# Triangular solve in a DeltaNet block: substitution on 16x16 blocks, joined by matrix products

## The chip, the cores and the metric

The kernel runs on one NeuronCore of a Trainium2 chip. The metric is the device time of one launch in microseconds (us); lower is better. The engines are TensorE (PE in the profile, with PEld for its weight loads), VectorE (DVE), ScalarE (ACT), GpSimd (POOL) and SyncE (SP), which issues most of the DMAs. Each engine works through its own instructions in a fixed order and waits on semaphores for the others.

## What is computed

The reference is one layer of a hybrid block: a gated DeltaNet branch and a Fourier branch over 256 tokens (with 256 context tokens before them), a merge, and a mixture of 32 experts. The change concerns one step of the DeltaNet branch. For every chunk of 64 tokens, every one of 8 heads and both directions, a unit lower triangular 64x64 matrix is solved:

```python
lower = jnp.where(strict, bc[..., :, None] * kk * decay, 0.0)
rhs = jnp.concatenate([bc[..., None] * vc, (bc * jnp.exp(gc))[..., None] * kc], axis=-1)
sol = lax.linalg.triangular_solve(jnp.eye(CHUNK) + lower, rhs, left_side=True, lower=True, unit_diagonal=True)
```

With 8 chunks, 8 heads and 2 directions that is 128 matrices. The kernel forms their inverses (transposed, the tiles `ub`) once, and the scan over the chunks then multiplies by them.

## The kernel before

The program goes through these stages: modulation and norm of the inputs (to about 60 us); the projections of the K heads, with their products and decays, which give the strictly triangular matrices in two pages `ah[0]` and `ah[1]`, one for each direction (to about 118 us); the projections of the eight V heads, beside which the triangular matrices are inverted; the four Q heads; the scan over 4 + 4 chunks, with the remaining projections (z, Fourier, gates) as fill between its steps; the merge; the router; and from about 470 us the experts, whose weights (3 x 32 matrices of 4 MB) stream in over the SP queue.

One V head (lines 557 to 571) takes one pass over four engines: ACT rounds the raw weights to `hi` (L156), POOL subtracts for `lo` (L157), PE makes 48 products into a bank `ps_pj` (L164 to L166; the pool has two such banks), ACT starts the convolution (L388), DVE adds its ten other taps (L391, called a tap below), ACT applies SiLU (L405), PE transposes in four pieces (L569), ACT copies them out (L571). A Q head does the same with 24 products and eight taps, and no transposes.

The inversion stands after the V heads in the code, and the scheduler that lays down the program mixes it into them. A 64x64 matrix is cut into four 32x32 blocks. L647 brings the two diagonal blocks of every matrix to one page `xc`, L649 transposes it in 32x32 blocks into `xt`, so that each of the 128 partitions holds two of the 32x32 triangles along its free dimension. The substitution (L651 to L657) then inverts them all at once in 31 steps; step s has two DVE instructions, each on two blocks of 31-s rows by s+1 columns:

```python
V.tensor_tensor(out=pv, in0=tt[:, :, s, 0:s + 1]..., in1=xt[:, :, s, s + 1:32]..., op=ALU.mult)   # L654
V.tensor_tensor(out=tv, in0=tv, in1=pv, op=ALU.subtract)                                         # L657
```

Four transposes (L672, L674) bring the inverses and their transposes back to `uc` (the page `xt`) and `tb` (the page `xc`). ACT spreads the diagonal blocks into `ub` (L678, eight copies). The off-diagonal 32x32 block is the product of three: for each half of the matrices (s = 0, 1), 64 small products of 32x32 (L688) go to a bank `ps_sc` (four such banks, shared with the transposes of the V heads), ACT copies with a minus sign to `yt` (L689), 64 more products (L696) follow, and DVE adds the result to `ub` (L699, twice). The products of the scan's first step (L745) read `ub`. A set below means 64 such small products.

What sets the order: each engine's order is fixed when the program is built. The program's scheduler chose it; buffers (two `ps_pj`, four `ps_sc`, three `a`) and data set when each instruction may start.

Of the kernel before, what the change touches and what calls it, by code (L numbers as in the profile page):

```python
# [14 lines left out]
AF = mybir.ActivationFunctionType  # L15
ALU = mybir.AluOpType
# [29 lines left out]
_o = 0  # L46
for _n, _w in (("ident", 128), ("before", 128), ("ones", 1), ("iota", 64), ("pid", 1),
               ("mle", 128), ("mge", 128), ("mgt", 128), ("mlt", 128), ("par0", 1), ("par1", 1), ("cgt", 64), ("clt", 64), ("ceq", 64),
               ("cle", 64), ("cge", 64), ("ev", 1), ("od", 1), ("sel", 32), ("cc", 128), ("sc", 128), ("cl", 1024)):
    _C[_n] = (_o, _w)  # L50
    _o += _w
NCST = _o
# [3 lines left out]
def _constants():  # L56
    a = np.zeros((128, NCST), np.float32)

    def put(n, v):
        o, w = _C[n]  # L60
        a[:, o:o + w] = v
# [17 lines left out]
    put("cge", tl >= j)  # L79
    put("ev", (t // 32) % 2 == 0)  # L80
    put("od", (t // 32) % 2 == 1)
    put("sel", (t % 32) == np.arange(32)[None, :])
    put("before", t < i)
    put("ones", 1.0)
# [13 lines left out]
def hybrid_block(es: ExitStack, tc: tile.TileContext, cst, x, c, ctx, c_ctx, w_mod, b_mod, norm1_g, norm2_g, w_in,  # L98
# [17 lines left out]
    def P(tag):  # L116
        return ps.tile([128, 512], F32, name="ps_" + tag, tag=tag, bufs=_nb[tag])
# [10 lines left out]
    def page(name, dtype=F32, tag="pg"):  # L128
        return pg.tile([128, 2048], dtype, name=name, tag=tag, bufs=NPG if tag == "pg" else 2)
# [306 lines left out]
    tt = page("tt").rearrange("p (d i c) -> p d i c", d=2, i=32)  # L436
    G.memset(tt.rearrange("p d i c -> p (d i c)"), 0.0)
    G.memset(tt.rearrange("p d i c -> p d (i c)")[:, :, 0:1024:33], 1.0)
# [201 lines left out]


    xc = page("xc").rearrange("p (d m j) -> p d m j", d=2, j=32)
    xt = page("xt").rearrange("p (d j i) -> p d j i", d=2, j=32)
    prod = page("prod")
    for d in range(2):
# [3 lines left out]
        V.transpose(xt[:, d].rearrange("p j i -> p (j i)") if d == 0 else xt[:, d].rearrange("p i j -> p j i"),  # L649
                    xc[:, d].rearrange("p m j -> p j m"))  # L650
    for s in range(31):  # L651
        n = 31 - s
        pv = prod[:, 0:2 * n * (s + 1)].rearrange("p (d i c) -> p d i c", d=2, i=n)
        V.tensor_tensor(out=pv, in0=tt[:, :, s, 0:s + 1].rearrange("p d (o c) -> p d o c", o=1).broadcast_to([128, 2, n, s + 1]),  # L654
                        in1=xt[:, :, s, s + 1:32].rearrange("p d (i o) -> p d i o", o=1).broadcast_to([128, 2, n, s + 1]), op=ALU.mult)
        tv = tt[:, :, s + 1:32, 0:s + 1]
        V.tensor_tensor(out=tv, in0=tv, in1=pv, op=ALU.subtract)  # L657

    take(fz, NZ)
# [4 lines left out]
    zT = page("zT", F32R).rearrange("p (q g t) -> p q g t", q=2, g=4)  # L664


    tb, yt = xc, prod[:, 0:1024].rearrange("p (m n) -> p m n", n=32)
    uc = xt.rearrange("p d j i -> p d (j i)").rearrange("p d (m i) -> p d m i", i=32)
    ub = [page("ub0").rearrange("p (d m n) -> p d m n", d=2, n=64), page("ub1").rearrange("p (d m n) -> p d m n", d=2, n=64)]
    vv = [(tt[:, d].rearrange("p i c -> p (i c)"), tt[:, d].rearrange("p i c -> p c i")) for d in range(2)]  # L670
    for d in range(2):
        V.transpose(uc[:, d].rearrange("p m i -> p i m"), vv[d][d])  # L672
    for d in range(2):
        V.transpose(tb[:, d].rearrange("p m c -> p c m"), vv[d][1 - d])  # L674
    for s in range(2):
        for d in range(2):
            for b in range(2):
                A.activation(ub[s][:, d, :, 32 * b:32 * b + 32], uc[:, d, 16 * s:16 * s + 16, :], AF.Copy, scale=par32[b])  # L678
    for s in range(2):
        p = P("sc")  # L680
        pv = p.rearrange("p (m n) -> p m n", n=32)
        for ml in range(16):
            m = 16 * s + ml
            for d in range(2):
                for hh in range(2):
                    k0 = 64 * hh + 32 * (1 - d)
                    o0 = 64 * hh + 32 * d
                    mm(pv[o0:o0 + 32, ml, :], ah[d][k0:k0 + 32, m, 32 * d:32 * d + 32], uc[k0:k0 + 32, d, m, :], start=True, stop=True)  # L688
        A.activation(yt[:, 16 * s:16 * s + 16, :], pv, AF.Copy, scale=-1.0)  # L689
        p = P("sc")  # L690
        pv = p.rearrange("p (m n) -> p m n", n=32)
        for ml in range(16):
            m = 16 * s + ml
            for q in range(4):
                r = slice(32 * q, 32 * q + 32)
                mm(pv[r, ml, :], tb[r, q % 2, m, :], yt[r, m, :], start=True, stop=True)  # L696
# [548 lines left out]
```

## Time and profile before

| | us |
|---|---|
| median of three runs | 1448.76 (1446.08 to 1449.28) |
| the profiled execution, its own time | 1448.83 |
| its span in the trace | 1446.9 |
| DVE busy over the span | 510.8 (35%) |
| PE busy over the span | 1303.9 (90%) |
| the 62 instructions of the substitution, L654 and L657, DVE busy | 48.7 |
| first product of the scan (L745) starts at | 224.7 |
| DMA moves 418 GB/s in the stretch | 470 to 1420 |

The profile says for each engine when it was busy, and for each wait what released it. A share over the whole span says little here, since the stages have different limits: the engine that sets the pace has to be read stage by stage.

### The profile page before, as it was taken

How to read it: one execution, taken by the hardware profiler on the slowest of the kernel's cores; microseconds unless marked ns; L12 is line 12 of the kernel's file. 1: busy time of each engine (PE TensorE's matmuls, PEld its weight loads, DVE VectorE, ACT ScalarE, POOL GpSimd, SP SyncE). 2: the span in 40 equal slices, each digit the busy share in tenths (PEclk: the TensorE clock that was granted, in tenths of full speed). 3: DMA queues.
4: the chain of work that ended last, by engine and by line, in shares of the span. 5: the costliest groups of instructions: out<-in, count | busy, mean ns of one | idle time of the engine just before them, and what ended most of it. 6: DMA issues, size and time to landing. Idle time of an engine off the chain costs nothing. (4 is left out here: it accounts for less than half of the span.)

```text
span 1446.9 us, 18887 instructions
## 1 busy us (share of the span) xinstructions
PE 1303.9 (90%) x7761; PEld 664.9 (46%) x7761; DVE 510.8 (35%) x965; ACT 243.7 (17%) x434; POOL 276.6 (19%) x256
## 2 busy tenths in 40 slices
PE   4997859899779889999999999999999999999996
PEld 2667858578569634333333333233333333333331
DVE  3579994655348411225112111211121112111213
ACT  3443333233224200000000000000000000000001
POOL 2434336544233130000100000001000000010000
PEclk9998979999879899999999999999999999999999
DMA  9962222124336999999999999999999999999994
GB/s 323 377 249 74 73 60 75 45 78 112 88 131 223 397 406 418 420 398 419 420 421 421 421 421 421 422 420 421 421 421 421 421 421 421 422 420 421 420 422 201
DMA packets 121159, 469.74 MB, mean 325 GB/s; under 512 B 10302, under 2 KB 63782, under 8 KB 69872
## 3 DMA queue, kind: packets, MB, share of 16 engines
q1 hardware_dynamic: 119696, 466.44, 81.0%
q10 hardware_dynamic: 1088, 1.89, 0.4%
q8 instruction: 62, 1.02, 0.3%
q0 software_dynamic: 288, 0.19, 0.2%
q14 instruction: 25, 0.20, 0.0%
HBM read 467.44 MB, written 1.05 MB: 324 GB/s over the span
## 5 line engine op out<-in xcount | busy, mean ns | idle before, releaser
L1111 PE MATMUL ps_gu<-we,xg 128*64 128x512 f32 x2048 | 469.6, 598 | 0.0
L1111 PEld LDWEIGHTS ps_gu<-we,xg 128*64 128x64 f32 x2048 | 141.2, 137 | 293.4 <-issue 280.2
L1134 PE MATMUL ps_dn<-we,aT 128*64 128x512 f32 x1024 | 237.3, 600 | 0.7 <-SPq L1146 0.4
L1100 POOL CAST rowsel<-pick 128x128 fp32r<-128x128 f32 x32 | 9.7, 304 | 684.5 <-PE ps_gu L1112 684.5
L157 POOL TENSOR_TENSOR lo<-raw,hi 128x1024 fp32r<-128x1024 f32 x44 | 106.3, 2418 | 157.6 <-ACT hi L156 123.2
L1143 DVE TENSOR_TENSOR x_pg<-x_pg,ps_st 128x512 f32<-128x512 f32 x128 | 82.6, 685 | 125.7 <-PE ps_st L1141 125.7
L1134 PEld LDWEIGHTS ps_dn<-we,aT 128*64 128x64 f32 x1024 | 66.9, 136 | 120.5 <-issue 113.7
L1117 ACT ACTIVATE sg<-gt 128x512 f32<-128x512 f32 x32 | 20.1, 629 | 448.1 <-DVE gt L1115 423.6
L1119 DVE TENSOR_SCALAR up<-ps_gu 128x512 f32<-128x512 f32 x32 | 22.1, 691 | 196.0 <-PE ps_gu L1112 189.2
L1137 DVE TENSOR_TENSOR ys<-ps_dn,g2r 128x512 f32<-128x512 f32 x32 | 22.1, 692 | 195.9 <-PE ps_dn L1134 195.9
L1141 PE MATMUL ps_st<-ys,wT 64*128 64x512 f32 x256 | 77.3, 641 | 12.8 <-DVE ys L1137 12.0
L156 ACT CAST hi<-raw 128x1024 fp32r<-128x1024 f32 x64 | 66.9, 1047 | 124.5 <-PE ps_pf L165 38.1
L164 PE MATMUL ps_pj<-u,hi 128*128 128x256 f32 x224 | 68.8, 310 | 18.1 <-DVE a L391 18.1
L1126 ACT COPY aT<-ps_tp 128x512 f32<-128x512 f32 x32 | 18.8, 586 | 322.0 <-PE ps_tp L1124 322.0
L1083 PEld LDWEIGHTS ps_tp<-oh,h 128*128 128x128 f32 x512 | 64.6, 201 | 14.1 <-issue 13.3
L391 DVE SCALAR_TENSOR_TENSOR a<-ps_pj,cvw,a 128x189 f32<-128x189 f32 (+3 forms) x152 | 63.8, 432 | 18.0 <-ACT a L388 16.3
L1083 PE MATMUL ps_tp<-oh,h 128*128 128x128 f32 x512 | 68.9, 290 | 1.1 <-DVE oh L1070 1.1
L1115 DVE TENSOR_SCALAR gt<-ps_gu 128x512 f32<-128x512 f32 x32 | 22.2, 692 | 133.2 <-issue 95.4
L165 PE MATMUL ps_pj<-u,hi 128*128 128x256 f32 x224 | 68.8, 308 | 0.0
L166 PE MATMUL ps_pj<-u,lo 128*128 128x256 f32 x224 | 67.2, 301 | 0.0
L1121 POOL TENSOR_TENSOR up<-up,sg 128x512 f32<-128x512 f32 x32 | 40.4, 1263 | 96.1 <-DVE up L1120 96.1
L164 PEld LDWEIGHTS ps_pj<-u,hi 128*128 128x128 f32 x224 | 46.0, 207 | 25.6 <-issue 23.8
(352 smaller groups left out, 1663.7 us busy)
## 6 DMA issues: line engine op xcount, KB each, us to landing
we<-in_w_gate_dram SPq DMA_DIRECT2D x128, 1024.0 KB, 18.4
we<-in_w_up_dram SPq DMA_DIRECT2D x128, 1024.0 KB, 17.8
we<-in_w_down_dram SPq DMA_DIRECT2D x128, 1024.0 KB, 18.9
raw<-in_w_in_dram SPq DMA_DIRECT2D x44, 512.0 KB, 4.0
wmb<-in_w_mod_dram SPq DMA_DIRECT2D x16, 1024.0 KB, 12.8
wm<-in_w_mod_dram SPq DMA_DIRECT2D x16, 512.0 KB, 8.1
raw<-in_w_gdn_out_dram SPq DMA_DIRECT2D x8, 512.0 KB, 4.1
raw<-in_w_merge_out_dram SPq DMA_DIRECT2D x8, 512.0 KB, 3.5
```

The lines of the kernel that those rows point to most:

```text
L156: A.copy(hi, r)
L157: eng.tensor_tensor(out=lo, in0=r, in1=hi.bitcast(F32), op=ALU.subtract)
L164: mm(out_, sh_, mh_, start=start and i == 0, stop=False)
L165: mm(out_, sh_, ml_, start=False, stop=False)
L166: mm(out_, sl_, mh_, start=False, stop=stop and i == n - 1)
L391: V.scalar_tensor_tensor(out=ov, in0=iv, scalar=wap, in1=ov, op0=ALU.mult, op1=ALU.add)
L1083: mm(p[:, kl * n:(kl + 1) * n], h2[:, t, rows2(k)], oh[:, n * t:n * t + n], start=(t == 0), stop=(t == 1))
L1111: mm(p[64 * g:64 * g + 64, :], xg[:, k, :], w[:, 512 * g:512 * g + 512], start=(k == 0), stop=False)
L1121: G.tensor_tensor(out=up, in0=up, in1=sg, op=ALU.mult)
L1134: mm(p[64 * g:64 * g + 64, :], aT[:, f % 4, 64 * (f // 4):64 * (f // 4) + 64], w[:, 512 * g:512 * g + 512], start=(f == 0), stop=(f == 7))
L1141: mm(p, wT[64 * g:64 * g + 64, t * 128:(t + 1) * 128], ys[64 * g:64 * g + 64, :], start=True, stop=True)
L1143: V.tensor_tensor(out=x_pg[:, t, gsl], in0=x_pg[:, t, gsl], in1=p, op=ALU.add)
```

## The change

The diagonal 32x32 blocks are cut again into four 16x16 blocks. The substitution runs on the 16x16 diagonal blocks, four in each partition, in 15 steps of two DVE instructions. Before it, two more DVE instructions bring the 16x16 diagonal blocks together (L658 of the new kernel) and two ACT instructions keep the off-diagonal ones in `aoff` (L661). After it, four transposes of half the size (L690, L694) are followed by four DVE and four ACT instructions that spread the inverses with masks (L691, L692, L697, L698). Then the off-diagonal 16x16 blocks are made by products, as those of 32x32 are already: for each half three more sets (`quarters`, L711), three ACT copies of the first set's result (L717, L720) and two DVE subtractions (L722, L724). The sets before (L688, L696) stay, with new names (L737, and L711 called from L739). Two mask columns are added to the constants.

```diff
-    for s in range(31):
-        n = 31 - s
-        pv = prod[:, 0:2 * n * (s + 1)].rearrange("p (d i c) -> p d i c", d=2, i=n)
+        V.scalar_tensor_tensor(out=xd[:, d], in0=xc[:, d, :, o:o + 16], scalar=(lo16, hi16)[d], in1=xc[:, d, :, 16 - o:32 - o],
+                               op0=ALU.mult, op1=ALU.add)
+        A.activation(aoff[:, :, o:o + 16], xc[:, d, :, o:o + 16], AF.Copy, scale=(hi16, lo16)[d])
+        V.transpose(xs[:, :, 0]... if d == 0 else xs[:, :, 1]..., xd[:, d].rearrange("p m j -> p j m"))
+    for s in range(15):
+        n = 15 - s
+        pv = tt[:, 1024:1024 + 4 * n * (s + 1)].rearrange("p (i b c) -> p i b c", i=n, b=4)
...
+    for d in range(2):
+        V.transpose(u16[:, d].rearrange("p m i -> p i m"), vv[d][d])
+        V.tensor_scalar_mul(uc[:, :, 1 + d, :], u16[:, d], (hi16, lo16)[d])
+        A.activation(uc[:, :, 3 * d, :], u16[:, d], AF.Copy, scale=(lo16, hi16)[d])
+    for d in range(2):
+        V.transpose(t16[:, d].rearrange("p m c -> p c m"), vv[d][1 - d])
+    for d in range(2):
+        V.tensor_scalar_mul(tbc[:, :, d, :], t16[:, d], (lo16, hi16)[d])
+        A.activation(tb[:, :, 1 + d, :], t16[:, d], AF.Copy, scale=(hi16, lo16)[d])
+    def quarters(s, lhs, rhs):
+        p = P("sc")
+        pv = p.rearrange("p (m n) -> p m n", n=32)
+        for ml in range(16):
+            for q in range(4):
+                r = slice(32 * q, 32 * q + 32)
+                mm(pv[r, ml, :], lhs(r, q, 16 * s + ml), rhs(r, 16 * s + ml), start=True, stop=True)
+        return pv
     for s in range(2):
+        pv = quarters(s, lambda r, q, m: aoff[r, m, :], lambda r, m: flat(uc)[r, m, 16:48])
+        A.copy(y16[:, ms_, :], pv)
+        for q in range(2):
+            A.copy(y16s[:, ms_, 16 - 16 * q:32 - 16 * q], pq[:, :, q, :])
+        pv = quarters(s, lambda r, q, m: flat(tbc)[r, m, :], lambda r, m: y16[r, m, :])
+        V.tensor_tensor(out=flat(uc)[:, ms_, 16:48], in0=flat(uc)[:, ms_, 16:48], in1=pv, op=ALU.subtract)
+        pv = quarters(s, lambda r, q, m: y16s[r, m, :], lambda r, m: flat(tbc)[r, m, :])
+        V.tensor_tensor(out=tb[:, ms_, 0:4:3, :], in0=tbc[:, ms_], in1=pv..., op=ALU.subtract)
```

How the instructions stand. DVE at the end of the substitution, before: every step's two instructions (L654, L657) have a tap (L391) between them, and the four transposes follow the last step. The program has 152 taps (40 for the K heads, 80 for the V heads, 32 for the Q heads, in about that order); 125 of them stand ahead of the transposes.

```order
L657 TENSOR_TENSOR tt<-tt,prod 128x2x2x30
L391 SCALAR_TENSOR_TENSOR a<-ps_pj,cvw,a 128x3x63
L654 TENSOR_TENSOR prod<-tt,xt 128x62
L391 SCALAR_TENSOR_TENSOR a<-ps_pj,cvw,a 128x4x63
L657 TENSOR_TENSOR tt<-tt,prod 128x2x31
L391 SCALAR_TENSOR_TENSOR a<-ps_pj,cvw,a 128x4x63
L672 STREAM_TRANSPOSE xt<-tt 128x32x32 x2
L674 STREAM_TRANSPOSE xc<-tt 128x32x32 x2
```

The same place on DVE now (taps are L393, the substitution is L668 and L671):

```order
L671 TENSOR_TENSOR tt<-tt 128x8x14
L393 SCALAR_TENSOR_TENSOR a<-ps_pj,cvw,a 128x192
L668 TENSOR_TENSOR tt<-tt,xt 128x60
L393 SCALAR_TENSOR_TENSOR a<-ps_pj,cvw,a 128x3x63
L671 TENSOR_TENSOR tt<-tt 128x4x15
L393 SCALAR_TENSOR_TENSOR a<-ps_pj,cvw,a 128x255
L690 STREAM_TRANSPOSE tt<-tt 128x16x32 x2
L694 STREAM_TRANSPOSE prod<-tt 128x16x32 x2
```

Ahead of the transposes there are now 91 taps. The last tap of the V heads is the 120th: the substitution ended four taps behind it, and ends thirty taps ahead of it now.

TensorE after the transposes of the last V head, before: two sets of one half (L696, of s = 0) and of the other (L688, of s = 1) stand together, ahead of them the first set and 34 products of projections; 24 more products and the last set follow, and then the scan's first product (L745).

```order
L166 MATMUL ps_pj<-u_156,lo 128x256
L164 MATMUL ps_pj<-u_156,hi 128x256
L696 MATMUL ps_sc<-prod,xc 32x32 x64
L688 MATMUL ps_sc<-xt,ah_446 32x32 x2
L688 MATMUL ps_sc<-xt,ah_447 32x32 x2
```

TensorE now, in the same stretch: three sets of 16x16 work stand together, the third of them of the other half.

```order
L168 MATMUL ps_pj<-u_157,lo 128x256
L166 MATMUL ps_pj<-u_156,hi 128x256
L711 MATMUL ps_sc<-tt 32x32 x64
L711 MATMUL ps_sc<-tt,prod 32x32 x64
L711 MATMUL ps_sc<-xt,prod 32x32 x64
L167 MATMUL ps_pj<-u_157,hi 128x256
```

Between the transposes of the last V head and the scan's first product there are now ten sets and 88 projection products (before: four sets and 58). Between the start of the V heads' stretch (the first product after the K heads' fill) and the scan's first product there are 469 projection products now and 442 before. All projections of the Q heads stand ahead of the scan now; 14 products of them stood behind its first product before.

## Rows read from the trace of the kernel before

**Rows 1.** Windows: us, busy PE, PEld, DVE, ACT, POOL, granted clock, DMA share, GB/s.

```profile
118.00:198.00 80.00, 58.39 (x416) 57.19 (x415) 78.09 (x142) 25.69 (x48) 31.21 (x25) 0.85 0.28 79
198.00:225.00 27.00, 17.52 (x579) 16.34 (x579) 19.52 (x31) 11.29 (x19) 9.08 (x5) 0.74 0.25 63
225.00:350.00 125.00, 121.13 (x1021) 93.38 (x1017) 67.32 (x193) 39.99 (x63) 71.61 (x49) 0.99 0.27 72
470.00:1420.00 950.00, 898.48 (x4198) 343.42 (x4196) 204.46 (x331) 74.21 (x133) 81.19 (x105) 0.99 1.01 418
```

**Rows 2.** Waits of PE, 118 to 226 us: total us, times, longest.

```profile
PE ps_pj L164 <- DVE a L391: 18.1, 5, 9.1
PE ps_sc L688 <- DVE xt L672: 5.8, 2, 4.3
```

**Rows 3.** Groups by line, 118 to 232 us: busy us, mean ns, idle before.

```profile
L391 DVE SCALAR_TENSOR_TENSOR a<-ps_pj,cvw,a 128x189 f32<-128x189 f32 (+3 forms) x100 | 41.4, 428 | 10.3 <-ACT a L388 9.6
...
L654 DVE TENSOR_TENSOR prod<-tt,xt 128x62 f32<-128x62 f32 (+15 forms) x31 | 25.0, 806 | 0.1
L657 DVE TENSOR_TENSOR tt<-tt,prod 128x62 f32<-128x62 f32 (+15 forms) x31 | 23.7, 763 | 0.2
```

**Rows 4.** Timeline of DVE and POOL: start us, us, instruction.

```profile
165.48 0.68 DVE L657 TENSOR_TENSOR tt<-tt,prod 128x512 f32<-128x512 f32 x1
...
166.47 2.53 DVE L654 TENSOR_TENSOR prod<-tt,xt 128x510 f32<-128x510 f32 x1
...
198.64 0.21 DVE L654 TENSOR_TENSOR prod<-tt,xt 128x62 f32<-128x62 f32 x1
...
199.16 2.37 DVE L657 TENSOR_TENSOR tt<-tt,prod 128x62 f32<-128x62 f32 x1
...
166.05 2.40 POOL L157 TENSOR_TENSOR lo<-raw,hi 128x1024 fp32r<-128x1024 f32 x1 [6.53 <-ACT hi L156]
```

**Rows 5.** DVE timeline, and the source view of L268 (ns min/median/max).

```profile
125.72 1.28 DVE L647 SCALAR_TENSOR_TENSOR xc<-ah,cs 128x1024 f32<-128x1024 f32 x1
...
128.43 4.25 DVE L649 STREAM_TRANSPOSE xt<-xc 128x1024 f32<-128x1024 f32 x2
...
201.84 3.72 DVE L672 STREAM_TRANSPOSE xt<-tt 128x1024 f32<-128x1024 f32 x2
...
L268 DVE TENSOR_SCALAR x_pg<-x_pg,rstd x2: 748/748/748, 20.1 to 20.8; 128x1024 f32<-128x1024 f32 x2
```

**Rows 6.** Timeline of PE; in brackets the idle time before and its releaser.

```profile
122.40 0.51 PE L164 MATMUL ps_pj<-u,hi 128*128 128x256 f32 x1 [4.27 <-DVE a L391]
...
197.86 0.60 PE L569 MATMUL ps_sc<-cs,b 128*128 128x128 f32 x4
...
205.61 1.92 PE L688 MATMUL ps_sc<-xt,ah 32*32 32x32 f32 x124 [1.50 <-DVE xt L672]
...
208.06 0.41 PE L164 MATMUL ps_pf<-hi,u 128*128 128x256 f32 x1
208.27 0.41 PE L165 MATMUL ps_pf<-lo,u 128*128 128x256 f32 x1
...
211.94 0.28 PE L164 MATMUL ps_pj<-u,hi 128*128 128x256 f32 x1
212.06 0.28 PE L165 MATMUL ps_pj<-u,hi 128*128 128x256 f32 x1
...
213.22 1.25 PE L696 MATMUL ps_sc<-prod,xc 32*32 32x32 f32 x126
...
216.24 1.12 PE L688 MATMUL ps_sc<-xt,ah 32*32 32x32 f32 x109 [1.58 <-issue]
...
224.70 1.87 PE L745 MATMUL ps_sc<-bv,ub 64*64 64x128 f32 x16
```

**Rows 7.** ACT: the source view of L678 (ns), and a copy of 256 elements.

```profile
L678 ACT ACTIVATE ub<-xt,cs x8: 706/708/723, 203.8 to 211.2; 128x512 f32<-128x512 f32 x8
...
195.27 0.37 ACT L571 COPY vtokc<-ps_sc 128x256 f32<-128x256 f32 x1
```

More of the change, by code (lines that the diff above doesn't have):

```diff
@@ L81, in _constants @@
     put("od", (t // 32) % 2 == 1)
+    put("lo16", (t // 16) % 2 == 0)
+    put("hi16", (t // 16) % 2 == 1)
     put("sel", (t % 32) == np.arange(32)[None, :])
@@ L435, in hybrid_block @@
     pkk = [P("sc"), P("sc")]
-    tt = page("tt").rearrange("p (d i c) -> p d i c", d=2, i=32)
-    G.memset(tt.rearrange("p d i c -> p (d i c)"), 0.0)
-    G.memset(tt.rearrange("p d i c -> p d (i c)")[:, :, 0:1024:33], 1.0)
+    tt = page("tt")
+    G.memset(tt[:, 0:1024], 0.0)
+    for q in range(4):
+        G.memset(tt[:, 16 * q:16 * q + 976:65], 1.0)
     for h in range(4):
@@ L642, in hybrid_block @@
     xc = page("xc").rearrange("p (d m j) -> p d m j", d=2, j=32)
-    xt = page("xt").rearrange("p (d j i) -> p d j i", d=2, j=32)
+    xt = page("xt")
     prod = page("prod")
+    lo16, hi16 = C("lo16"), C("hi16")
+    xd = xt[:, 0:1024].rearrange("p (d m j) -> p d m j", d=2, j=16)
+    xs = xt[:, 1024:2048].rearrange("p (s d a i) -> p s d a i", s=16, d=2, a=2)
+    aoff = prod[:, 0:1024].rearrange("p (m j) -> p m j", j=32)
     for d in range(2):
@@ L664, in hybrid_block @@
     zT = page("zT", F32R).rearrange("p (q g t) -> p q g t", q=2, g=4)
-    tb, yt = xc, prod[:, 0:1024].rearrange("p (m n) -> p m n", n=32)
-    uc = xt.rearrange("p d j i -> p d (j i)").rearrange("p d (m i) -> p d m i", i=32)
+    td = [tt[:, 0:1024].rearrange("p (i d a c) -> p d i a c", i=16, d=2, a=2)[:, d] for d in range(2)]
+    vv = [(v.rearrange("p i a c -> p i (a c)"), v.rearrange("p i a c -> p c a i")) for v in td]
+    u16 = tt[:, 1024:2048].rearrange("p (d m i) -> p d m i", d=2, i=16)
@@ new lines, in hybrid_block, with flat @@
+    yt = prod[:, 1024:2048].rearrange("p (m n) -> p m n", n=32)
+    def flat(v):
+        return v.rearrange("p m q i -> p m (q i)")
+    def quarters(s, lhs, rhs):
+        p = P("sc")
+        pv = p.rearrange("p (m n) -> p m n", n=32)
+        for ml in range(16):
+            for q in range(4):
+                r = slice(32 * q, 32 * q + 32)
+                mm(pv[r, ml, :], lhs(r, q, 16 * s + ml), rhs(r, 16 * s + ml), start=True, stop=True)
+        return pv
+    for s in range(2):
+        ms_ = slice(16 * s, 16 * s + 16)
+        pv = quarters(s, lambda r, q, m: aoff[r, m, :], lambda r, m: flat(uc)[r, m, 16:48])
+        A.copy(y16[:, ms_, :], pv)
+        pq = pv.rearrange("p m (q i) -> p m q i", q=2)
+        for q in range(2):
[3 more added lines that the diff above has]
+        pv = quarters(s, lambda r, q, m: y16s[r, m, :], lambda r, m: flat(tbc)[r, m, :])
+        V.tensor_tensor(out=tb[:, ms_, 0:4:3, :], in0=tbc[:, ms_], in1=pv.rearrange("p m (q i) -> p m q i", q=2), op=ALU.subtract)
@@ L676, in hybrid_block @@
         for d in range(2):
             for b in range(2):
[L678 removed]
+                A.activation(ub[s][:, d, :, 32 * b:32 * b + 32], flat(uc)[:, ms_, 32 * d:32 * d + 32], AF.Copy, scale=par32[b])
     for s in range(2):
@@ L687, in hybrid_block @@
                     o0 = 64 * hh + 32 * d
-                    mm(pv[o0:o0 + 32, ml, :], ah[d][k0:k0 + 32, m, 32 * d:32 * d + 32], uc[k0:k0 + 32, d, m, :], start=True, stop=True)
+                    mm(pv[o0:o0 + 32, ml, :], ah[d][k0:k0 + 32, m, 32 * d:32 * d + 32], flat(uc)[k0:k0 + 32, m, 32 * d:32 * d + 32], start=True, stop=True)
         A.activation(yt[:, 16 * s:16 * s + 16, :], pv, AF.Copy, scale=-1.0)
[L690 to L696, printed above, removed]
+        pv = quarters(s, lambda r, q, m: flat(tb)[r, m, 32 * (q % 2):32 * (q % 2) + 32], lambda r, m: yt[r, m, :])
         for d in range(2):
```

22 lines of the change are left out of this document (13 added, 9 removed).

## The prediction

> **What bounds the kernel now.** I read the windows first, because every stage has its own limit. From 470 to 1420 us the DMA engines are full and move 418 GB/s [rows 1]: that is the stream of expert weights. Nothing of it is changed, so whatever happens ahead moves it as a whole, and a microsecond won or lost before the scan should come out at the end as one. The second thing to see is the row from 118 to 198 us, where the V heads and the substitution run together: DVE is busy for 78.1 of 80 us, PE for 58.4, and PE's clock is granted at 0.85. From 198 to 225 DVE has 19.5 of 27 us and PE 17.5 at 0.74. From 225 to 350 it is PE that is full, 121 of 125 us. So up to 198 us DVE sets the pace. The waits say the same: PE stood 18.1 us for taps (a bank of ps_pj comes free when the taps have read it) and 5.8 us for the transposes behind the substitution [rows 2]. The groups show what DVE does there: 41.4 us for 100 taps, and 25.0 + 23.7 = 48.7 us of substitution [rows 3].
>
> **What a substitution step costs.** Two undisturbed rows give the price of a DVE instruction on two SBUF tiles: 62 elements take 0.21 us and 512 take 0.68 [rows 4]. That is 1.04 ns for an element and 0.145 us for an instruction. The 31 steps have 2 x 10,912 = 21,824 elements in 62 instructions: 22.8 + 9.0 = 31.8 us. The trace has 48.7. The other 16.9 us are stalls: a product of 510 elements took 2.53 us while POOL ran L157 from 166.05 to 168.45, and the last subtraction, of 62 elements, took 2.37 [rows 4]. Eleven instructions of the substitution are stretched like these two, 1.5 us each on average, one for each spell of POOL work beside it. The taps, whose other operand is in PSUM, show no such stretch: 428 ns on average [rows 3].
>
> **The change on DVE.** The 15 steps have 2 x 2,720 = 5,440 elements in 30 instructions: 5.7 + 4.3 = 10.0 us. Their stalls depend on how much POOL work falls beside them. There are 31 taps between the steps (12.7 us), so the stretch is some 28 us long where it was 69, and four of the eleven spells of POOL fall into it: 6 us, with 3 and 9 as bounds. New are two passes of 512 elements (L658; half of 1.28 each by L647's row, 1.3 us [rows 5]) and four masks of 512 elements (the nearest row is 0.75 for 1024 on SBUF alone [rows 5]; between 0.38 and 0.75 each, and I take 0.42, nearer to half, 1.7 us). The transposes are of half the size: the two ahead save half of 4.25, 2.1 us, and the four behind cost twice half of 3.72, 3.7 us [rows 5]. The four subtractions L722 and L724 come after the V heads and are in the tail below.
>
> I follow this to the last tap of the V heads, since in either order the small products stand behind the transposes of the last V head on PE. Before, DVE reached the transposes L672 at 201.84 us [rows 5], with five taps of the Q heads already made. Now: 201.8 - 48.7 + 10.0 + 6.0 (stalls) - 2.1 (five taps of 0.41) + 1.3 + 1.7 + 3.7 - 2.1 = 171.6 us for the last V tap, if DVE never waits. PE has a floor of its own: it starts again at 122.40, and 381 projection products at 0.12 us (the spacing of 211.94 and 212.06) and eight groups of transposes at 0.6 are 50.5 us; two stretches of 16 products at 0.21 us (the spacing of 208.06 and 208.27), as PE's restarts show them, add 3 [rows 6]: 176 us. A V head passes PE (5.7 us), ACT and DVE (4.1 us of taps and its share of the steps) with two banks between them, so two floors so close don't overlap fully. I add 2 us (bounds 0 and 6): the last V tap at 178. SiLU follows (0.7 by the nearest ACT row of 512 elements [rows 7]), and ahead of the transposes PE now has 21 products of a Q head, which wait for the bank that the last V tap frees (2.5 us): **the last V transposes at 181 us, 17 before 197.86.**
>
> The page "SBUF — State Buffer" of the Trainium skill (section "Who interferes with whom") says that a DVE instruction with two SBUF inputs contends with a GpSimd instruction that reads SBUF, as the stretched rows show, and that tensor_scalar on SBUF can too, which speaks against this change: it adds four of those and two passes with two SBUF inputs. No row here has a tensor_scalar beside a busy POOL. By the page one or two more stalls of 1.5 us would come on top, and DVE's floor would be 174.
>
> **The change in the tail,** from there to the scan's first product, which started at 224.70 [rows 6]: 26.8 us before. Its work at full clock is 58 products at 0.12 us and four sets at 1.15 (1.12 and 1.25 us for 109 and 126 of a set's 128 records [rows 6]): 11.6 us. Of the other 15.2 us, 5.8 are the wait for the end of the substitution [rows 2], 1.6 a wait inside the chain of sets [rows 6], and 7.8 are half clock and smaller waits: products 0.21 us apart, and the set at 205.61 that took 1.92 [rows 6]. Now there are 88 products and ten sets: 10.6 + 11.5 = 22.1 us at full clock. The 5.8 go, because the substitution is done thirty taps earlier. I keep the 7.8. The 1.6 goes or stays with the order; the chain of a half has two more passes from PE over ACT or DVE and back, with projections laid between them, and I take 1.2 for all of it. ACT's part of that chain is 1.45 us for the three copies (0.71 at most for 512 elements, 0.37 for 256 [rows 7]) beside products on PE. Sum: 31 us, so **the scan's first product at 212 us, 12.7 earlier.** The bounds of the tail are 24 (22.1 and 2 of half clock) and 42 (all 88 products at 0.21 and all sets at 1.92, 37.7, and 4 of waits).
>
> The scan then has less to share PE with: 469 projection products stand before it and not 442, and PE is full to 350 us [rows 1], so 27 x 0.12 = 3.2 us more are saved there. ACT's other new work (six masks at 0.71 us, 4.2 us [rows 7]) lies in a stretch where it is busy 25.7 of 80 us [rows 1]; if that cover were gone it would cost those 4.2. POOL's memsets and the two mask columns lie at the start of the program, and no wait that I read ends with them.
>
> **The sum.** 12.7 + 3.2 = 16 us. The profiled execution took 1448.83 us (span 1446.9, and 1.9 around it), within 0.1 of the median of the runs, 1448.76. Forecast: **1433 us.** With the good bounds (overlap 0, no slow restarts of PE, tail 24) the gain is 16 + 2 + 3 + 7 = 28: 1421. With the bad ones (overlap 6, tail 42) it is 16 - 4 - 11 = 1: 1448.
>
> **Rivals.**
> 1. The tail runs like PE at its best, and DVE's relief comes through whole: a tail of 24 to 26 us, gain 21 to 28, about 1425. For it speaks that the wait for the substitution is gone and that the gaps in the chain have products laid into them. Against it, the sets of before stand next to waits and slow products [rows 6].
> 2. Half clock through the whole tail. The granted clock is 0.74 from 198 to 225 us [rows 1], with four sets; now ten stand there. All at the slow prices: 37.7 + 2 = 40 us, the scan at 221, gain 3.7 + 3.2 = 7: 1442. The Trainium skill, page "TensorE: Matmul & The Clock Gate", section "A second HAM failure mode: psum-queue depth-cycling", tells of a kernel whose short idle spells between groups of matmuls, as it cycled through PSUM banks, made the clock swing between its two levels. By that rule this rival is the outcome.
> 3. Slower than before: the sets become a serial chain through ACT and DVE, with one half in front of the other in ACT's fixed order (the four spreads of `ub` for s = 1 stand ahead of `yt` for s = 0). Price: every set costs what the dearest one cost with its wait, 1.92 + 1.50 [rows 6]; ten of them and 88 slow products are 53 us, the scan starts at 234, 9 later, and after the 3.2 the time is 1455. It decides from a tail of about 47 us on. Against it: that set waited for the end of the substitution, which is out of the way now.
> 4. The V heads were never held by DVE's load but by their own chain through four engines; then their end moves by less than 5 us, and the longer tail takes it: within 0.2% of 1449. Against it stands DVE's 78.1 of 80 us.
>
> **How the numbers follow.** Chances: the forecast (1427 to 1439) 0.48, rival 1 0.22, rival 2 0.17, rival 3 0.08, rival 4 0.05. The range leaves out the far end of rival 2 and rivals 3 and 4: 1421 to 1445. A measurement of this kernel can tell about 0.2% (3 us) from no change. Faster by more than that: 0.48 + 0.22 + most of rival 2 = 0.86. Within: 0.06, rival 4 and a remainder of rival 2. Slower: 0.08, rival 3.
>
> **What would show it.** Right: L668 and L671 together 13 to 19 us busy; PE's wait for taps well under 18.1 us; the last V transposes near 181 and the scan's first product near 212; the stream of expert weights full 16 us earlier and as long as before. Wrong: a substitution above 22 us (more stalls); the V heads ending after 188; a tail above 40 us with a granted clock near 0.5; or a scan that starts earlier and a stream that starts when it did.

## The result, and the profile after

The changed kernel takes 1454.19 us (1451.24 to 1457.94) beside 1444.41 us (1439.30 to 1449.28) of the kernel before on the same chip: the ratio is 1.0066, interval 1.0053 to 1.0078. It is slower by about 10 us where 16 us of gain were forecast. The execution that was profiled took 1454.31 us, with a span of 1452.3; the profiled execution of before (span 1446.9) was one of the slower of its kernel, so the two traces differ by less, 5.4 us, than the medians do.

The windows, with the same columns as [rows 1], show first that VectorE was relieved as meant: 59.8 us of the 80 up to 198, where it had 78.1. Behind it, from 198 to 225, PE has half as many matmuls again (895 where it had 579) in about the same busy time, at the same low granted clock. The row between is the tail of the changed kernel, from the last V transposes to the scan's first product.

```profile
118.00:198.00 80.00, 62.27 (x725) 60.93 (x726) 59.81 (x131) 33.22 (x62) 34.33 (x23) 0.89 0.31 84
198.00:225.00 27.00, 18.42 (x895) 17.45 (x895) 10.80 (x23) 10.17 (x19) 4.77 (x2) 0.75 0.22 61
190.12:232.37 42.25, 30.50 (x1374) 28.87 (x1372) 14.16 (x30) 15.46 (x28) 11.58 (x6) 0.80 0.16 43
225.00:350.00 125.00, 118.49 (x1102) 91.08 (x1102) 60.69 (x175) 37.83 (x59) 69.13 (x48) 0.97 0.23 64
470.00:1420.00 950.00, 898.25 (x4208) 345.30 (x4207) 206.77 (x334) 75.03 (x134) 81.72 (x105) 0.99 1.01 418
```

The groups of DVE in the changed kernel from 118 to 198 us (busy us, mean ns, idle before and its releaser) answer to [rows 3]: the substitution is 9.0 + 6.9 = 15.9 us. The taps now wait for ScalarE: 19.0 us in this stretch, where it was 1.4 us before.

```profile
L393 DVE SCALAR_TENSOR_TENSOR a<-ps_pj,cvw,a 128x189 f32<-128x189 f32 (+3 forms) x86 | 35.4, 431 | 20.0 <-ACT a L390 19.0
L668 DVE TENSOR_TENSOR tt<-tt,xt 128x60 f32<-128x60 f32 (+7 forms) x15 | 9.0, 601 | 0.1
L671 DVE TENSOR_TENSOR tt<-tt 128x60 f32<-128x60 f32 (+7 forms) x15 | 6.9, 459 | 0.1
```

PE's waits in the same stretch, as in [rows 2], which go to 226 us (behind 198 no further one for taps came): there are still waits for taps, 11.9 us where it had 18.1.

```profile
PE ps_pj L166 <- DVE a L393: 11.9, 3, 5.4
PE ps_pj L166 <- DVE tt L671: 3.6, 1, 3.6
```

And PE's timeline in the tail, as in [rows 6] (in brackets the idle time ahead of a row, and what ended it). L711 are the sets of the first join and the last sets of the second, L737 the first sets of the second:

```profile
190.12 0.60 PE L573 MATMUL ps_sc<-cs,b 128*128 128x128 f32 x4
190.65 1.29 PE L711 MATMUL ps_sc<-xt,prod 32*32 32x32 f32 x128
...
194.99 1.25 PE L711 MATMUL ps_sc<-tt 32*32 32x32 f32 x126
...
198.69 0.99 PE L711 MATMUL ps_sc<-tt,prod 32*32 32x32 f32 x95 [2.16 <-issue]
...
202.70 1.51 PE L711 MATMUL ps_sc<-xt,prod 32*32 32x32 f32 x97 [2.73 <-issue]
...
209.87 1.18 PE L711 MATMUL ps_sc<-tt,prod 32*32 32x32 f32 x117 [0.33 <-issue]
...
214.42 1.82 PE L737 MATMUL ps_sc<-xt,ah 32*32 32x32 f32 x119 [3.28 <-issue]
...
226.71 0.31 PE L737 MATMUL ps_sc<-xt,ah 32*32 32x32 f32 x12 [3.25 <-issue]
...
232.37 1.09 PE L788 MATMUL ps_sc<-bv,ub 64*64 64x128 f32 x16
```

Two things are to be seen. The last V transposes stand at 190.12 us, 7.7 earlier than in [rows 6] and not 17. And the tail lasts 42.25 us where before it lasted 26.8, so the scan starts at 232.37, 7.7 later. Five pauses, 11.75 us together, stand in it. None has a semaphore behind it ("issue"), and none stands between two sets, where a set would wait for ScalarE or VectorE: each cuts a set in two. Between the pauses at 198.69 and 202.70 one set's worth of records runs. The kernel before had two such pauses, the 1.58 us in [rows 6] and this one:

```profile
224.52 0.25 PE L696 MATMUL ps_sc<-prod,xc 32*32 32x32 f32 x5 [1.44 <-issue]
```

The page of the profile has a line that fits: a queue that carries nothing but instructions. Before, it was 62 packets, and the whole program had 18,887 instructions. Now it is 68, for 1,536 instructions more, which are six blocks of 256; a packet is 16 KB.

```profile
span 1452.3 us, 20423 instructions
...
q8 instruction: 68, 1.11, 0.3%
```

A set is 64 products of 4 TensorE instructions each (two weight loads, two matmuls, so 128 MATMUL records): 256 instructions, one such packet. The queue is TensorE's: its matmuls and weight loads together are 15,522 instructions before and 17,058 now, 60.6 and 66.6 blocks of 256, and in every kernel below the packets are these blocks, rounded up, and one more. The times of the packets in the traces say the same: in the thirteen kernels of this case PE has 53 pauses without a semaphore between 118 us and the scan, and each of them ends 1.15 to 1.58 us after a packet of this queue has landed. The stream of expert weights starts 5.9 us later (first load at 427.8 us, before 421.9) and is about as long as before (956.7 us from its first load of gate weights to the last, 955.7 before), as the prediction had it.

### The profile page after: what moved, and what is told of

It reads as the page before. It is cut to its first block, busy times and chain, and to the rows that moved or that the text cites. A ratio compares the mean times of both kernels' runs of the same rounds, so it can differ in the third digit from the quotient of the medians.

```text
span 1452.3 us, 20423 instructions
## 1 busy us (share of the span) xinstructions
PE 1311.0 (90%) x8529; PEld 670.5 (46%) x8529; DVE 478.2 (33%) x943; ACT 251.6 (17%) x447; POOL 277.8 (19%) x259
## 5 line engine op out<-in xcount | busy, mean ns | idle before, releaser
L166 PE MATMUL ps_pj<-u,hi 128*128 128x256 f32 x224 | 68.6, 309 | 15.5 <-DVE a L393 11.9
L393 DVE SCALAR_TENSOR_TENSOR a<-ps_pj,cvw,a 128x189 f32<-128x189 f32 (+3 forms) x152 | 63.4, 433 | 39.9 <-ACT a L390 37.8
L166 PEld LDWEIGHTS ps_pj<-u,hi 128*128 128x128 f32 x224 | 45.6, 205 | 24.5 <-issue 24.5
```

The lines of the kernel that those rows point to most:

```text
L166: mm(out_, sh_, mh_, start=start and i == 0, stop=False)
L393: V.scalar_tensor_tensor(out=ov, in0=iv, scalar=wap, in1=ov, op0=ALU.mult, op1=ALU.add)
```

## Experiments

Three theories were put up. **T1, instruction supply:** TensorE gets its instructions in blocks of 256, and rows of small products use a block up sooner than the next one comes. **T2, hops:** the sets wait for copies and subtractions on ScalarE and VectorE. **T3, half clock.** The table has, for each kernel, the ratio to the kernel before on the same chip, and from its profiled execution the last V transposes, the scan's first product, what lies between, the pauses of PE without a semaphore in that stretch, and how many projection products stand in it. The scheduler lays out each kernel anew, so these products are not the same in number, and a tail is to be compared with them in mind (0.12 us each at full clock).

| kernel | ratio (95%) | V transposes | scan | between | pauses | products |
|---|---|---|---|---|---|---|
| before | 1 | 197.86 | 224.70 | 26.84 | 3.0 | 58 |
| changed | 1.0066 (1.0053 to 1.0078) | 190.12 | 232.37 | 42.25 | 11.8 | 88 |
| b_small | 1.0154 (1.0116 to 1.0191) | 197.94 | 245.15 | 47.21 | 12.5 | 63 |
| b_wide | 1.0028 (1.0009 to 1.0048) | 199.21 | 229.14 | 29.93 | 2.7 | 63 |
| a_cut | 1.0065 (1.0041 to 1.0088) | 191.30 | 228.63 | 37.33 | 14.7 | 42 |
| a_wide | 0.9950 (0.9934 to 0.9965) | 191.12 | 220.60 | 29.48 | 2.7 | 112 |
| a_nojoin | 0.9924 (0.9895 to 0.9954) | 195.08 | 209.13 | 14.05 | 1.9 | 50 |
| b_nosub | 0.9871 (0.9852 to 0.9890) | 186.78 | 202.56 | 15.78 | 2.5 | 50 |
| a_eight | 0.9999 (0.9980 to 1.0018) | 192.05 | 228.14 | 36.09 | 10.3 | 96 |

### Six idle sets, small and wide

The kernel before with six more sets that nobody reads, ahead of its own four; once with small products (b_small), once with the same columns in a quarter of the instructions (b_wide).

```diff
+    for s in range(6):
+        pv = P("sc").rearrange("p (m n) -> p m n", n=32)
+        for ml in range(16):
+            for q in range(4):
+                r = slice(32 * q, 32 * q + 32)
+                mm(pv[r, ml, :], tb[r, 0, ml, :], uc[r, 0, ml, :], start=True, stop=True)
```

```diff
...
+        for ml in range(4):
+            for q in range(4):
+                r = slice(32 * q, 32 * q + 32)
+                mm(p[r, 128 * ml:128 * ml + 128], tb[r, 0, ml, :], uc[r, 0, 4 * ml:4 * ml + 4, :]..., start=True, stop=True)
```

> The kernel before, with six further sets of 64 products of 32x32 laid ahead of its own four, in one row of 384 products on TensorE, on operands that are ready (the inverses and their transposes after the substitution); nobody reads their results, the output is the same. Theory T1, TensorE's instruction supply: a set is 256 TensorE instructions (two weight loads and two matmuls for each product), and of these no more than one set's worth arrives each 4 us once a row of sets is longer than what was fetched ahead; so the six sets take 16 to 24 us, with pauses of about 2.7 us inside the row, with no semaphore behind them, and the scan's first product moves from 224.7 to 240 to 248 us; total +15 to +23 us. Theory T2, the hops over ScalarE and VectorE are what made the tail long: these sets wait for nobody, so they take 1.15 to 1.92 us each, 7 to 11 in all, without a pause; total +7 to +11. Theory T3, half clock: the same 11 us, at a granted clock near 0.5.

> The same as the run with six more sets of small products, with the same columns in a quarter of the instructions: each of the six sets is 16 products of 32x32 by 32x128, 64 TensorE instructions and not 256; nobody reads the results. T1 (instruction supply): the six sets are 1.5 sets' worth of instructions and take 5 to 10 us with at most one pause; total +5 to +10, less than half of the run with small products. T2 and T3 (hops, half clock): the row costs the same in both runs, 7 to 11 us, since columns, banks and waits are the same.

PE's timeline of b_small, the six sets (768 records):

```profile
207.78 2.22 PE L684 MATMUL ps_sc<-xt,xc 32*32 32x32 f32 x160 [2.19 <-DVE xc L674]
211.48 1.93 PE L684 MATMUL ps_sc<-xt,xc 32*32 32x32 f32 x128 [1.47 <-issue]
215.48 1.93 PE L684 MATMUL ps_sc<-xt,xc 32*32 32x32 f32 x128 [2.08 <-issue]
218.81 1.93 PE L684 MATMUL ps_sc<-xt,xc 32*32 32x32 f32 x128 [1.40 <-issue]
222.27 1.93 PE L684 MATMUL ps_sc<-xt,xc 32*32 32x32 f32 x128 [1.52 <-issue]
225.72 1.38 PE L684 MATMUL ps_sc<-xt,xc 32*32 32x32 f32 x85 [1.52 <-issue]
```

From pause to pause exactly 128 records run, one block, whatever set they belong to (the last 85 go on into the next set), and a block comes each 3.3 to 4.0 us. DMA in the same 19 us (GB/s in 40 slices, then the queue: packets, MB, share): the pulses are the blocks, six of them; nothing else moves but one packet of another instruction queue. A block is not slow for its bytes: the share, 1.9% of 16 engines over 19.08 us, is 0.97 us for each packet, and PE goes on 1.3 to 1.5 us after it has landed.

```profile
GB/s 0 0 34 0 0 0 0 0 0 0 0 34 0 0 17 0 0 0 34 0 0 0 0 0 0 34 0 0 0 0 0 0 34 0 0 0 0 0 0 34
...
q8 instruction: 6, 0.10, 1.9%
```

The wide row of b_wide (192 records) starts like that:

```profile
209.06 6.78 PE L684 MATMUL ps_sc<-xt,xc 32*32 32x128 f32 x180 [2.05 <-DVE xc L674]
```

It runs without a pause. The same columns took 19.1 us as small products (207.78 to 226.87) and 6.5 us as wide ones (209.06 to 215.58), and the total rose by 22 us in the one case and by 4 in the other. T1 said 16 to 24 us for the small row and 15 to 23 for the total, and both came; for the wide one it said 5 to 10 for both, and the row took that while the total rose by less. No set here waits for another engine, so T2 has no part in these 22 us. Half clock was there: the granted clock is 0.51 over the small row and 0.74 over the wide one, and 128 records took 1.93 us where they take 1.29 at full clock. But it doesn't set the time of the row: blocks came 3.3 to 4.0 us apart at half clock here, and 4.0 us apart between 198.69 and 202.70 in the changed kernel, where the 128 records ran in 1.3 us. So T3 is not the cause.

### The chain cut, and the chain kept with fewer instructions

In a_cut the second and third set of each half read pages that are ready. In a_wide all waits are kept, and a set of the first join is 64 instructions.

```diff
-        pv = quarters(s, lambda r, q, m: flat(tbc)[r, m, :], lambda r, m: y16[r, m, :])
+        pv = quarters(s, lambda r, q, m: flat(tbc)[r, m, :], lambda r, m: flat(tbc)[r, m, :])
...
-        pv = quarters(s, lambda r, q, m: y16s[r, m, :], lambda r, m: flat(tbc)[r, m, :])
+        pv = quarters(s, lambda r, q, m: flat(tbc)[r, m, :], lambda r, m: flat(tbc)[r, m, :])
```

```diff
...
+        for ml in range(0, 16, 4):
+            for q in range(4):
+                r = slice(32 * q, 32 * q + 32)
+                mm(pv[r, ml:ml + 4, :], lhs(r, q, 16 * s + ml), rhs(r, slice(16 * s + ml, 16 * s + ml + 4)), start=True, stop=True)
```

> The changed kernel with the chain of the first join cut: the second and third set of each half read a page that is ready (the masked transposes) in place of the copies y16 and y16s, so no set of the first join waits for a copy of ScalarE. All sets, copies and subtractions are still made; the inverses are wrong by this. Seven sets now stand in a row behind the transposes of the last V head. T1 (instruction supply): the seven sets take 24 to 28 us, pauses of 2.5 to 3 us stand inside the sets as before, the tail from the last V transposes to the scan's first product stays at 38 to 46 us and the scan starts at 228 to 236. T2 (hops): the pauses go; seven sets take 8 to 13 us, the tail falls to 28 to 31 us and the scan starts near 220. T3 (half clock): seven sets of 1.92, 13.5 us, at a clock near 0.5.

> The changed kernel with each of the six sets of the first join made of 16 products of 32x32 by 32x128 in place of 64 products of 32x32 by 32x32: the same columns, banks, copies, subtractions and waits for them, in 64 TensorE instructions and not 256 (four matrices share one left operand, so the inverses are wrong). T1 (instruction supply): the tail from the last V transposes to the scan's first product falls from 42 to 22 to 27 us, no pause without a semaphore stands in the first join, and the total is 15 to 20 us below that of the changed kernel. T2 (hops over ScalarE and VectorE): all hops are still there, so the tail stays at 38 us or more and the total within 4 us of the changed kernel's.

PE's timeline of a_cut, inside the row of seven sets:

```profile
196.35 1.30 PE L711 MATMUL ps_sc<-tt 32*32 32x32 f32 x128 [2.65 <-issue]
200.35 1.17 PE L711 MATMUL ps_sc<-tt 32*32 32x32 f32 x70 [2.70 <-issue]
...
208.11 1.93 PE L711 MATMUL ps_sc<-tt 32*32 32x32 f32 x128 [1.95 <-issue]
...
215.29 1.19 PE L737 MATMUL ps_sc<-xt,ah 32*32 32x32 f32 x73 [1.61 <-issue]
```

The chain is gone and the pauses are not: 14.7 us of them. The six sets of the first join and the one of the second behind them took 24.5 us (191.92 to 216.41), in T1's 24 to 28 and far from T2's 8 to 13. The tail is 37.3 us, a little under T1's 38 to 46: it has 46 projection products fewer than the changed kernel's, 5.5 us at full clock, which stand behind the scan's first product here. So the scan starts 3.7 us sooner and the stream of expert weights doesn't (first load at 431.0 us, 427.8 in the changed kernel), and the total is that of the changed kernel.

PE's timeline of a_wide, three sets of the first join and the only long pause, in a set of the second join, which is small products still:

```profile
195.83 1.07 PE L711 MATMUL ps_sc<-tt 32*32 32x128 f32 x32
196.73 1.05 PE L711 MATMUL ps_sc<-tt,prod 32*32 32x128 f32 x32
197.60 1.05 PE L711 MATMUL ps_sc<-xt,prod 32*32 32x128 f32 x32
...
214.32 1.60 PE L746 MATMUL ps_sc<-xt,ah 32*32 32x32 f32 x100 [2.73 <-issue]
```

With every hop in place the tail falls from 42.25 to 29.5 us, though it has 24 projection products more (2.9 us). T1 had 22 to 27, T2 38 or more. The ratio falls from 1.0066 to 0.9950, 17 us, in T1's 15 to 20. So what makes the first join dear is the number of its TensorE instructions; the hops and what half clock there is are in the 29.5.

### What the relief of VectorE is worth

a_nojoin leaves out the first join's sets, copies and subtractions and keeps the shorter substitution; b_nosub is the kernel before without the 31 steps.

```diff
-        pv = quarters(s, lambda r, q, m: aoff[r, m, :], lambda r, m: flat(uc)[r, m, 16:48])
...
-        V.tensor_tensor(out=tb[:, ms_, 0:4:3, :], in0=tbc[:, ms_], in1=pv..., op=ALU.subtract)
```

```diff
-    for s in range(31):
...
-        V.tensor_tensor(out=tv, in0=tv, in1=pv, op=ALU.subtract)
```

> The changed kernel without its first join: the three sets, three copies and two subtractions of each half are left out (the off-diagonal 16x16 blocks of the inverses are wrong by this); the shorter substitution, the masks and the four sets of the second join stay. It shows what the relief of VectorE is worth by itself. Expected by all theories: the last V transposes at 189 to 191 us as in the changed kernel. T1 (instruction supply): four sets are four blocks of instructions, the tail is 16 to 20 us, the scan starts at 206 to 210 and the total is 14 to 18 below that of before. T2 (hops): the hops of the second join stay, the tail is 20 to 23 us, the scan starts at 210 to 213, 11 to 14 below. If the last V transposes come at 181 or sooner, VectorE and not the V heads' own chain was delayed by the join's work.

> The kernel before without its substitution: the 31 steps are left out (the inverses are wrong), all else stays. VectorE loses its whole 48.7 us. Theory D (the V heads end when VectorE has no more to do, as the prediction had it): the last V transposes move from 197.9 to 176 to 181 us, TensorE's floor. Theory C (from some load on the V heads are held by their own chain: products, ScalarE's rounding and SiLU in a fixed order, taps, two banks): they end at 186 to 195 us, as in the changed kernel and in the one without the first join (190 and 195), although VectorE has 33 us less to do than in the changed kernel.

Without the join the tail is 14.05 us and the total 11 us below before. The scan's start, 209.1, lies in T1's range, but by another way: the V heads end at 195.08, later than the 189 to 191 that all theories had, for a reason that no run shows, and the tail is shorter than the 16 to 20. The total lies in T2's range (11 to 14 below) and not in T1's (14 to 18), so this run does not choose between the two. Beside the changed kernel six sets and 38 projection products (4.6 us) make 28.2 us of tail: 3.9 us a set. That is the price of a block in the row of b_small.

In b_nosub, PE's last V transposes, its wait for taps from 118 to 200 us, and the engines' busy time to the end of the V heads (columns as in [rows 1]):

```profile
186.78 0.60 PE L569 MATMUL ps_sc<-cs,b 128*128 128x128 f32 x4
```

```profile
PE ps_pj L164 <- DVE a L391: 15.4, 3, 10.1
```

```profile
118.00:187.00 69.00, 53.55 (x424) 52.99 (x423) 48.04 (x89) 31.13 (x56) 29.48 (x25) 0.90 0.29 84
```

VectorE has no substitution at all and is busy for 48 of 69 us, and the V heads end at 186.8 us, not at 176 to 181; PE waits 15.4 us for taps all the same. The taps in turn waited 19.5 us for ScalarE's first step of the convolution (L388), and ScalarE 14.3 us for PE's transposes (L569). So theory D is out and C came as expected: from some load on the V heads are held by their own chain, in which each engine waits for another. Which link of it is the one to mend, no run shows. Of the 11 us between 197.9 and 186.8 the change had got 7.7.

### The sets laid among projections

If blocks come each 3.3 to 4.0 us, a set costs less where projection products, 0.12 us each with two instructions, run between sets. Two orders were tried: the substitution ahead of V head 4 in the code, and one set behind each 24 projection products from some point on (`tick` takes the next set with its copies; a_spread11 has 11 for the 9).

```diff
+    def tick():
+        slot[0] += 1
+        if slot[0] > 9 and slot[0] % 1 == 0:
+            take(jn[0])
...
             proj(p[:, 256 * s:256 * s + 256], w, s)
+            tick()
...
+    fq = fill_q()
+    for _ in range(4):
+        take(fq)
+        tick()
...
-    fill = chain(fill_q(), fz, fill_gates())
+    fill = chain(fq, fz, fill_gates())
```

> The changed kernel with the same work in another order: substitution and join stand in the code ahead of the last V heads, and each of the ten sets is laid behind 24 projection products of the heads V4 to V7 and Q0 to Q3, so that on TensorE one or at most two sets stand together from 168 us on, with about 20 products between them. T1 (instruction supply): the blocks of instructions of a set arrive while products run; the ten sets cost 12 to 20 us and not 42, the scan starts at 206 to 216 us in place of 232.4 and the total is 8 to 18 us below that of before. T2 (hops): the hops have products beside them as well, so the same order gains; the difference is in the pauses: by T1 those without a semaphore stand only where two sets adjoin, by T2 there are none.

> As the run before with the sets laid in two V-head slots later: the first set stands at about 170 us, the last two before the scan have 25 products between them. T1: within 5 us of the run before; scan at 206 to 220, total 5 to 17 us below that of before. If both orders give no more than the changed kernel, the tail's length is not set by how the sets stand among the products.

Both were slower than before: 1.0090 (1.0067 to 1.0113) and 1.0062 (1.0038 to 1.0085). The scan started at 222.0 and 221.5 us, ten earlier than in the changed kernel, but later than the 206 to 216 (and 220) expected. By the last sentence of the second expectation this speaks against T1, and it wants a reason. Pauses of 10.0 and 7.8 us remained between 118 us and the scan, some in single sets with 20 products ahead of them: 20 products and a set are 296 instructions, in 3.6 us, so that the blocks can't get ahead. And the rest was lost behind the scan's start: of 400 to 425 us PE was busy for 6.0 us in a_spread9, before for 14.3. There the diff had a side effect: with the four Q heads taken out of `fill`, each step of the scan took its other fill four pieces sooner. One line undoes that:

```diff
-    fill = chain(fq, fz, fill_gates())
+    fill = chain(iter(range(4)), fq, fz, fill_gates())
```

> The run with ten spread sets (first of the two orders) with one difference: the scan's steps take the same projections as fill as in the changed kernel. There the four Q heads had been taken ahead and each step of the scan then took its fill four pieces sooner, so that the fill ran out before the scan did. Theory F: that is why a scan that started 2.7 us earlier than before ended later; with the fill in its old steps the stream of expert weights starts 2 to 5 us earlier than in the kernel before and the total is 2 to 6 us below it. If the total stays 10 us above before, the fill is not the reason.

The loads of the gate weights on the SP queue (ns min/median/max, first and last start in us), a_spread9 and then a_spread_fill:

```profile
L877 SPq DMA_DIRECT2D we<-in_w_gate_dram x128: 327/328/727, 430.0 to 1387.7; - x128
```

```profile
L877 SPq DMA_DIRECT2D we<-in_w_gate_dram x128: 327/328/713, 418.6 to 1371.0; - x128
```

The stream starts 11.4 us sooner by that line (the scan itself started 2.7 us sooner, at 219.3). The ratio is 0.9982 (0.9963 to 1.0001), 2.6 us below before, inside the 2 to 6 expected, though the interval reaches to no change. That is still less than the 8 to 18 that T1 had promised for this order: 9.8 us of pauses are left.

### Eight sets, and eight sets spread

The third set of a half makes the transpose of what the second made. VectorE, idle in the tail, can transpose it.

```diff
-            A.copy(y16s[:, ms_, 16 - 16 * q:32 - 16 * q], pq[:, :, q, :])
...
-        pv = quarters(s, lambda r, q, m: y16s[r, m, :], lambda r, m: flat(tbc)[r, m, :])
-        V.tensor_tensor(out=tb[:, ms_, 0:4:3, :], in0=tbc[:, ms_], in1=pv..., op=ALU.subtract)
+        V.transpose(flat(tb)[:, ms_, :].rearrange("p m (d n) -> p (m d) n", d=2), flat(uc)[:, ms_, :]...)
```

> The changed kernel with eight sets in place of ten and the same result: the third set of each half of the first join (which makes the transposed block) is replaced by a transpose in 32x32 blocks on VectorE from what the second set gave, so two sets (512 TensorE instructions), their two subtractions, four copies and two masks on ScalarE fall away and two transposes of 1024 elements, 1.9 us each, come in. Order of the code as in the changed kernel. T1 (instruction supply, about 4 us for each set): the tail falls by 7 to 8 us to 34 or 35, the scan starts at 224 to 226 and the total is 6 to 9 us below the changed kernel's, level with the kernel before. T2 (the sets' own products and hops): two sets of 1.2 to 1.9 us are 2.4 to 3.8 us less.

> Eight sets as in the run before, laid among the projections of the last V heads and the Q heads: single sets with about 24 products between them from 166 us on; the projections that fill the scan stand in the scan's steps as in the changed kernel. T1: eight sets and the 190 products between them are some 9.5 blocks of instructions; at 3.7 us a block they need 35 us, of which the V heads' own time covers most; the scan starts at 208 to 216 us and the total is 8 to 16 us below that of before. If the scan starts there and the total is not below before, the loss lies behind the scan's start, in the fill.

a_eight is level with before (0.9999), 0.67% or 9.7 us below the changed kernel, where T1 had 6 to 9. Its profiled tail is 36.1 us: 6.2 less, where T1 had 7 to 8 and T2 at most 3.8; it has eight projection products more. Laid among the projections with the fill kept in its steps, a_eight_spread takes 1434.23 us (1432.99 to 1435.98), a ratio of 0.9930 (0.9908 to 0.9952): 10 us below before, faster than both kernels, with the same result. Its PE timeline has 3.2 us of pauses left ahead of the scan:

```profile
183.13 1.29 PE L633 MATMUL ps_sc<-tt 32*32 32x32 f32 x128
...
186.63 1.14 PE L658 MATMUL ps_sc<-xt,ah 32*32 32x32 f32 x110 [0.98 <-issue]
...
194.86 1.29 PE L633 MATMUL ps_sc<-prod,xc 32*32 32x32 f32 x128
...
204.62 0.60 PE L679 MATMUL ps_sc<-cs,b 128*128 128x128 f32 x4
205.15 1.29 PE L658 MATMUL ps_sc<-xt,ah 32*32 32x32 f32 x128
...
209.50 1.29 PE L633 MATMUL ps_sc<-prod,xc 32*32 32x32 f32 x128
...
213.72 1.09 PE L804 MATMUL ps_sc<-bv,ub 64*64 64x128 f32 x16
```

The sets stand alone or in twos and run in 1.2 us each, two of the eight with a pause inside. The V heads end later (204.62), since they share PE with the sets, and only two sets are left behind them: the scan starts at 213.7 us, in the expected 208 to 216, and the gain is in the expected 8 to 16.

## Why the prediction was wrong

1. **The substitution: right.** 10.0 and six of stalls were forecast, 16 us (13 to 19); L668 and L671 took 15.9. By the prices of the prediction 5.9 of that are stalls, nearly all in five instructions that ran while POOL was busy, so the mechanism is right too.
2. **That the stream of expert weights moves as a whole: right.** It starts 5.9 us later, the span ends 5.4 later. Of the 3.2 us for 27 products more ahead of the scan 2.3 came in these two executions (the scan started 7.7 later); the medians are 9.8 us apart, so whether they came at all is not shown.
3. **The end of the V heads: mis-sized.** 181 us were forecast and 190.1 came. The two floors (VectorE done by 172 us, PE by 176) are not what held. The term that failed is "I add 2 us (bounds 0 and 6)" for the chain of a V head between them: it would have had to be 11. PE started again at 119.43 us, 3.0 earlier than in the floor, but from there on it waited 5.36, 1.06, 3.60, 0.65 and 4.16 us, 14.8 together, and after the three long waits some 60 products ran at half clock and not 32. b_nosub shows the size of that chain with no substitution on VectorE: 186.8 us, so about 10 us behind PE's floor. Rival 4 named this mechanism at 0.05, though its "never" is too strong: the relief of VectorE moved the end by 7.7 us, where it had less than 5.
4. **The tail: the step that turned the sign.** Forecast 31 us, 29.9 of work and half clock and 1.2 for "all of" the waits in the chain of sets. Measured: 42.25, with 11.75 us of pauses; without them 30.5. So the sum of work and half clock came out (some of that is luck: the 7.8 us of half clock were carried over from a tail of four sets, with a pause of 1.44 us in it), and the pauses were ten times the 1.2. The step that failed is that term: a supply of instructions stood nowhere in the sum. The clue stood in the rows: the wait of 1.58 us in [rows 6] is "issue", in the middle of a set, with no semaphore, and I read it as "a wait inside the chain of sets". It was one block of instructions that had not come: a packet of 16 KB started at 213.67 us and took 1.23, and PE went on 1.3 us after it had landed. Four sets among 58 products paused for 3.0 us; ten sets, some of them in rows of three, for 11.75.
5. **The rivals.** Rival 3 had the sign and, at 1455 us, the time, by a chain through ScalarE and VectorE; that chain is not the cause (a_cut, a_wide). Its tail of 53 us from 181 on did not come either: 42.25 us came, under the 47 from which it was to decide, from 190.1 on, so the time agrees by luck. Its price of 1.92 + 1.50 us for a set, the second number a wait for another engine, is near the 3.3 to 4.0 us of a block by chance. Rival 2 had a tail of 40 us, near the one that came, but by half clock through the whole of it, and that did not come: the granted clock in it is 0.80, and its products stand 0.12 us apart in some stretches and 0.21 in others.
6. **Summed:** the V heads 9.1 us and the tail 11.3 us worse than forecast are 20.4, which is the scan at 232.4 for 212. By the medians the forecast was 25.7 us off; the rest is 0.9 of the 3.2 us, and 4.4 by which the profiled execution of before stood above the median beside the changed kernel.

The Trainium skill, page "Runtime: NRT & Kernel Launch", section "Instruction fetch mechanics", tells that an engine's instructions are refilled in blocks of 16 KiB, 256 instructions, and that crossing into the next is mostly hidden. The first agrees with the 16 KB packets and the 128 records from pause to pause. The second doesn't hold here: a row of sets used a block up in 1.2 to 1.9 us and got one each 3.3 to 4.0. Most of that time is not the packet's own (about 1 us): in b_small the next packet started 1.1 to 1.6 us after PE had gone on, and PE went on 1.3 to 1.5 us after it had landed. What fixes these two, and how many blocks are fetched ahead (160 records in b_small and 184 in a_cut ran before the first pause), stays open.

## What to carry to other kernels

Count TensorE's instructions as well as its columns: here a row of products so small that 256 instructions run in 1.2 us paid 3.3 to 4.0 us for each 256, whatever it waited for otherwise. An idle time marked "issue" in the middle of a set, with a packet of the instruction queue beside it, was that in every case here; it went with fewer, wider products (b_wide, a_wide), and for the most part with fewer sets and long products laid between them (a_eight_spread). And an engine at 78 of 80 us of load is worth relieving only down to the next chain: run the kernel once without the work (b_nosub) to see where that is.

## What the runs showed that was not expected

A projection product of 256 columns has two instructions and takes 0.12 us, a small product has four: one set needs a block of instructions in the time of ten projection products. A transpose of 1024 elements, 1.86 us (half of 3.72) in [rows 5] before, took 1.24 us in a_eight, where it reads 32x32 blocks that lie in a row; the layout is the one difference between them that I know of. And a change of the fill's place in the code moved the stream of weights by 11.4 us, of which 2.7 were there at the scan's start.
